# A mixture-of-experts kernel on one core: the last two experts' rows are added to gathered sums and written over the normalised output, an 87-row expert comes last, capacities are finer and expert 1 takes the unsplit path

## The chip, the cores and the metric

The kernel runs on one core of one Trainium2 chip. The metric is the device time of one execution in microseconds (us); the time before is the median of three runs.

## What is computed

One encoder layer runs over two sequences of 1024 and 512 tokens with 1024 features, in fp32: RMSNorm, one projection, a pooling mixer and differential attention, an output projection with a residual, and then a mixture of experts. Every token takes one of four groups and in it two of eight experts, 32 experts in all; an expert's three matrices are 1024x512 (gate, up) and 512x1024 (down).

```python
gates = g_top * (e_top / jnp.sum(e_top, axis=-1, keepdims=True))
eid = g_idx * EXPERTS_PER_GROUP + e_loc
...
hid = jax.nn.silu(xblk @ w_gate[e]) * (xblk @ w_up[e])
return hid @ w_down[e]
...
return h + ff                  # encoder_layer
x = rmsnorm(x, g_final)        # run_trunk, over each token's row
```

With the inputs that are drawn here, experts 0 and 1 get 146 and 41 rows (a row is one token of one expert); the other 30 get, sorted, 249, 248, 203, 195, 185, 158, 149, 139, 124, 106, 103, 97, 87, 84, 75, 71, 66, 61, 59, 58, 55, 53, 52, 49, 46, 33, 27, 24, 19 and 10.

## The kernel before, in words

The first half (mixer, attention, output projection, routing) is not touched. The routing leaves three arrays in DRAM: `hn` (the normalised rows), `acc` (the sums, which start as h) and `tab` (for each expert its tokens and gates).

**The expert stage** (`experts`, L1289) goes through 32 slots. Slots 0 and 1 are experts 0 and 1; behind them `ORDER` lists places in the sorted list of the other 30, the fullest being place 0. `CAPS` gives each place a capacity, that is, how many rows are gathered, multiplied and scattered whatever the true count; what goes over it would be done in extra passes (the loop at L1496), of which there are none here. A capacity is cut into blocks of at most 128 rows. In iteration i the tensor engine (PE) does gate(i), up(i) and down(i-1) (`use`, with `E.proj` L1067 and `E.down` L1078). Weights come in pieces of 1 MB, six for an expert, through eight buffers (`er_raw`) on SP's queue, up to eight pieces ahead.

A capacity of at most `WHOLE` = 64 takes the **whole** path: the weights go unsplit into fp32 matmuls, two side by side in the array's columns (0 and 64), and the two halves are added afterwards. All others are **split**: ACT copies a piece to a rounded high part (L104), DVE subtracts to get the low part (L108), and PE makes three passes (L112 to L114) for a block of over 64 rows, or two (L1113, L1114) for a smaller one. So a matrix costs PE the same time at 96 rows as at 128.

`gather` (L1145) fetches a block's rows from `hn` with an indirect DMA on POOL's queue, two experts ahead. `weigh` (L1187) scales the result by the gate; `scatter` (L1203) adds it to `acc` with an indirect DMA.

**The end** (`close`, L1223). The last `TAIL` = 2 experts (32 rows each) don't reach `acc` in time. Their weighted rows are split in high and low parts and stacked in one tile of 128 rows (`stack`). `tail_step` loads `acc` in six pieces (L1361) behind the last scatter of the third-last expert, and builds a 0/1 matrix `hot` of rows against all 1536 tokens (L1347, L1356). For each of twelve token tiles PE multiplies `hot` with the rows (L1232), DVE adds the product to the sums in two halves (L1236), ACT squares (L1238), the inverse root is taken on POOL for three groups and on DVE for the last, the row is scaled (L1256 on DVE; L1253 on ACT and L1254 on POOL for three tiles) and written out (L1259).

Of the kernel before, what the change touches and what calls it, by code (L numbers as in the profile page):

```python
# [1090 lines left out]
class Block:  # L1091
# [111 lines left out]
    def scatter(self):  # L1203
        self.nc.gpsimd.indirect_dma_start(out=self.E.S["acc"],  # L1204
                                          out_offset=bass.IndirectOffsetOnAxis(ap=self.ix[:self.m, 0:1], axis=0),
                                          in_=self.y[:self.m], in_offset=None, compute_op=OP.add)

    def stack(self, ps, parts):

        self.weigh(ps)  # L1210
        hi, lo = parts[:self.m], parts[self.m:]
        for hf in range(2):
            s = slice(hf * 512, (hf + 1) * 512)
            split_hi(self.nc, hi[:, s], self.y[:self.m, s])
            split_lo(self.nc, lo[:, s], self.y[:self.m, s], hi[:, s])
# [7 lines left out]
def close(nc, E, tail, outs):  # L1223

    accs, gB = tail["acc"], tail["g"]
    stat = E.X([128, FF], F32, "s", bufs=4)
    ss, rr, rt = (stat[:, i * TT:(i + 1) * TT] for i in range(3))

    def add(t):
        ps = [E.bank() for _ in range(2)]  # L1230
        for hf, p in enumerate(ps):
            nc.tensor.matmul(p, lhsT=tail["hot"][:, t * 128:(t + 1) * 128],  # L1232
                             rhs=tail["rows"][:, hf * 512:(hf + 1) * 512], start=True, stop=True)
        for hf, p in enumerate(ps):
            d = accs[t][:, hf * 512:(hf + 1) * 512]
            nc.vector.tensor_tensor(d, d, p, OP.add)  # L1236
            yield
        nc.scalar.activation(E.W([128, D], F32R, "hi"), accs[t], AF.Square, accum_out=ss[:, t:t + 1])  # L1238

    def root(ts, eng):  # L1240
        ts = slice(ts.start, ts.stop)
        if eng is nc.gpsimd:
            eng.tensor_scalar(ss[:, ts], ss[:, ts], 1.0 / D, EPS, op0=OP.mult, op1=OP.add)
            rsqrt_pool(nc, rr[:, ts], ss[:, ts], rt[:, ts])
            return
        nc.vector.tensor_scalar(ss[:, ts], ss[:, ts], 1.0 / D, EPS, op0=OP.mult, op1=OP.add)
        yield
        yield from rsqrt_steps(nc, rr[:, ts], ss[:, ts], rt[:, ts])

    def scale(t):  # L1250
        a, r = accs[t], rr[:, t:t + 1]
        if t in POOLED:
            nc.scalar.activation(a, a, AF.Copy, scale=r)  # L1253
            nc.gpsimd.tensor_tensor(a, a, gB, OP.mult)  # L1254
        else:
            nc.vector.scalar_tensor_tensor(a, a, r, gB, op0=OP.mult, op1=OP.mult)  # L1256
        tok = TGORDER[t // 4] * 512 + t % 4 * 128
        o, row = (outs[0], tok) if tok < NP else (outs[1], tok - NP)
        nc.sync.dma_start(o[row:row + 128], a)  # L1259
        yield  # L1260

    def run(work, side):
        for k, w in enumerate(work):
            for _ in w:
                for _ in range(SIDE if k else 0):
                    next(side, None)
        for _ in side:
            pass

    t0, ready, side = 0, [], iter(())  # L1270
    for w, e in zip(LAST, ROOTS):
        ts = range(t0, t0 + w)
        t0 += w
        run([add(t) for t in ts], side)
        side = root(ts, nc.gpsimd if e else nc.vector)
        if e:
            for _ in side:
                pass
        if t0 < TT:
            run([scale(t) for t in ready], iter(()))  # L1280
        else:
            run([iter(())] + [scale(t) for t in ready], side)
        ready = ts
    run([scale(t) for t in ready], iter(()))
    for b in tail["last"]:
        b.scatter()


def experts(tc, A, S, K, RO, outs):  # L1289
    nc = tc.nc  # L1290
    E = Experts(tc, A, S, K)
    with ExitStack() as ctx:
# [16 lines left out]
        def ids(i):  # L1309
# [33 lines left out]
        def tail_step(k):  # L1343
            if k == 0:
                assert all(b.m == 128 // TAIL // 2 for b in tail["last"])
                tail["pos"] = E.raw()[:, :NT]
                nc.gpsimd.iota(tail["pos"], pattern=[[1, NT]], base=128, channel_multiplier=0,  # L1347
                               allow_small_or_imprecise_dtypes=True)
                tail["g"] = E.rows()
                nc.sync.dma_start(tail["g"], bcast(A["g_final"], D))  # L1350
                tail["to"] = E.X([128, 1], F32, "to")
                nc.vector.tensor_copy(tail["to"], tail["ix"][:, 0:1])
                tail["acc"] = []
            elif k == 1:
                tail["hot"] = E.raw()[:, :NT].bitcast(F32R)
                nc.vector.tensor_scalar(tail["hot"], tail["pos"], tail["to"], None, op0=OP.is_equal)  # L1356
                tail["rows"] = E.rows().bitcast(F32R)
            elif k <= 1 + TT // 2:
                a = E.raw().rearrange("p (t n) -> p t n", t=2)
                o = 128 + (k - 2) * 256  # L1360
                nc.sync.dma_start(a, S["acc"][o:o + 256].rearrange("(t p) n -> p t n", p=128))  # L1361
                tail["acc"] += [a[:, 0], a[:, 1]]
# [24 lines left out]
        def after(d, fn):  # L1387
            todo.append([d, fn])
# [60 lines left out]
        for i in range(n + 1):  # L1449
# [134 lines left out]
```

## Time and profile before

| | us |
|---|---|
| median of three runs (1427.0, 1428.17, 1430.35) | 1428.17 |
| the profiled execution, own time | 1432.71 |
| its span, first to last instruction | 1430.4 |
| PE busy in the span | 1328.7 (93%) |
| DVE, ACT, POOL busy | 828.1, 674.1, 230.4 |
| moved by DMA | 337.94 MB |

The span is what the profile's rows are placed in; the execution's own time holds 2.3 us more around it. A busy share is a mean over stages that have different limits, so rows are read by stage: the expert stage lies at about 700 to 1374 us of the span, the end behind it.

### The profile page before, as it was taken

To read this page: it belongs to the slowest core of one execution; us is meant where nothing else is said; L and a number is where in the kernel's file an instruction comes from. 1 tells how busy PE (TensorE), PEld (TensorE's weight loads), DVE (VectorE), ACT (ScalarE), POOL (GpSimd) and SP (SyncE) were. 2 spreads that over 40 slices of the span, in tenths; PEclk is the share of its full clock that TensorE was granted. 3 is DMA by queue.
4 is the path that set the end of the run, shared out by engine and by line. 5 is a ranking of instruction groups with operands and counts; after the bars stand their busy time and mean duration, and the time that the engine had idled before them with its cause. 6 is when DMAs were issued, how large, how long until landed. Compare 5 with 4: busy or idle time off the path is not lost.

```text
span 1430.4 us, 17564 instructions
## 1 busy us (share of the span) xinstructions
PE 1328.7 (93%) x5986; PEld 926.4 (65%) x5986; DVE 828.1 (58%) x1363; ACT 674.1 (47%) x1039; POOL 230.4 (16%) x376
## 2 busy tenths in 40 slices
PE   7899999988999999998789999999999999999970
PEld 5768888856676668776566656656565666677620
DVE  5495653066988727564766455263444665778354
ACT  6321212166877723221446455363535564777351
POOL 0000000003342210211212111110111122121032
PEclk9999999999999999999799999999999999999985
DMA  8625425436551048312498999898999999999674
GB/s 290 222 103 203 147 103 141 95 77 159 152 136 37 29 170 280 113 60 96 177 365 320 362 325 395 299 383 285 373 368 306 390 364 348 358 386 375 221 281 155
DMA packets 90347, 337.94 MB, mean 236 GB/s; under 512 B 17616, under 2 KB 25296, under 8 KB 65680
## 3 DMA queue, kind: packets, MB, share of 16 engines
q1 hardware_dynamic: 80368, 302.95, 58.3%
q0 software_dynamic: 9312, 29.65, 8.5%
q10 hardware_dynamic: 576, 4.19, 0.8%
q8 instruction: 48, 0.79, 0.2%
q14 instruction: 43, 0.35, 0.1%
HBM read 282.69 MB, written 54.06 MB: 235 GB/s over the span
## 4 chain that ended last, share of the span: by engine, by line
PE 78%; DMA 9%; DVE 5%; ACT 3%; POOL 2%; issue 2%; SPq 0%; POOLq 0%; ACTq 0%; DVEq 0%
PE pm_m L112 8%; PE pm_m L114 8%; PE pm_m L113 8%; PE pm_m L1071 6%; PE pz_z L113 5%; PE pz_z L112 5%; PE pz_z L114 5%; PE ps_sc L393 5%; PE po_o L451 4%; PE pt_t L1129 3%; DMA er_raw<-w_gate 3%; PE ph_h L114 3%; PE ph_h L112 3%; PE ph_h L113 3%; PE pm_m L1083 2%; PE pt_t L438 2%
## 5 line engine op out<-in xcount | busy, mean ns | idle before, releaser
L108 DVE TENSOR_TENSOR ew_lo<-er_raw,ew_hi 128x1024 fp32r<-128x1024 f32 x228 | 272.5, 1219 | 140.9 <-ACT ew_hi L104 140.4
L104 ACT ACTIVATE ew_hi<-er_raw 128x1024 fp32r<-128x1024 f32 x228 | 233.6, 1051 | 45.4 <-DMA er_raw<-w_gate 17.1
L112 PE MATMUL pm_m<-ew_hi,ex_x 128*128 128x512 f32 (+1 forms) x368 | 150.7, 410 | 0.2 <-ACT ex_x L1138 0.2
L113 PE MATMUL pm_m<-ew_lo,ex_x 128*128 128x512 f32 (+1 forms) x368 | 146.8, 399 | 0.0
L114 PE MATMUL pm_m<-ew_hi,ex_x 128*128 128x512 f32 (+1 forms) x368 | 146.6, 398 | 0.2 <-DVE ex_x L1139 0.2
L1204 POOL DMA_INDIRECT acc<-ex_y,ex_ix x40 | 71.7, 1792 | 322.2 <-ACT ex_y L1198 145.9
L112 PE MATMUL pz_z<-xT_hi,w_hi 128*128 128x512 f32 x288 | 115.3, 401 | 8.4 <-ACT xT_hi L153 8.4
L113 PE MATMUL pz_z<-xT_lo,w_hi 128*128 128x512 f32 x288 | 115.3, 401 | 0.0
L114 PE MATMUL pz_z<-xT_hi,w_lo 128*128 128x512 f32 x288 | 113.5, 394 | 0.0
L393 PE MATMUL ps_sc<-st_st 128*128 128x512 f32 x320 | 98.6, 449 | 6.9 <-ACT sm_e L412 5.6
L1071 PE MATMUL pm_m<-er_raw,ex_x 128*64 128x512 f32 (+1 forms) x416 | 96.3, 599 | 0.0
L408 ACT ACTIVATE sm_e<-ps_sc,sb_m 128x1024 f32<-128x1024 f32 x64 | 70.8, 1112 | 38.7 <-PE pt_t L438 37.3
L393 PEld LDWEIGHTS ps_sc<-st_st 128*128 128x128 f32 x320 | 60.5, 196 | 42.7 <-ACT sm_e L408 12.3
L397 DVE TENSOR_REDUCE sb_m<-ps_sc 128x1 f32<-128x1024 f32 x64 | 75.3, 1218 | 21.6 <-PE ps_sc L393 21.6
L112 PEld LDWEIGHTS pm_m<-ew_hi,ex_x 128*128 128x128 f32 (+1 forms) x368 | 66.6, 181 | 32.3 <-ACT ex_x L1138 7.3
L114 PEld LDWEIGHTS pm_m<-ew_hi,ex_x 128*128 128x128 f32 (+1 forms) x368 | 66.6, 181 | 21.1 <-DVE ex_x L1139 0.8
L113 PEld LDWEIGHTS pm_m<-ew_lo,ex_x 128*128 128x128 f32 (+1 forms) x368 | 66.8, 182 | 18.0 <-issue 0.2
L112 PE MATMUL ph_h<-wo_woh,mx_mh 128*128 128x512 f32 x192 | 77.8, 407 | 0.0
L114 PE MATMUL ph_h<-wo_woh,mx_ml 128*128 128x512 f32 x192 | 77.3, 403 | 0.0
L451 PE MATMUL po_o<-wT_wT,v_V 128*128 128x512 f32 x160 | 77.2, 606 | 0.0
L113 PE MATMUL ph_h<-wo_wol,mx_mh 128*128 128x512 f32 x192 | 77.2, 403 | 0.0
L112 PE MATMUL pm_m<-ew_hi,ex_h 128*128 128x512 f32 (+1 forms) x184 | 75.0, 408 | 0.0
(289 smaller groups left out, 2399.8 us busy)
## 6 DMA issues: line engine op xcount, KB each, us to landing
er_raw<-w_gate SPq DMA_DIRECT2D x64, 1024.0 KB
er_raw<-w_up SPq DMA_DIRECT2D x62, 1024.0 KB
er_raw<-w_down SPq DMA_DIRECT2D x62, 1024.0 KB
st_st<-qk SPq DMA_DIRECT2D x48, 256.0 KB
rw_raw<-w_in SPq DMA_DIRECT2D x16, 512.0 KB
rw_raw<-xT SPq DMA_DIRECT2D x12, 512.0 KB
x_x<-x SPq DMA_DIRECT2D x12, 512.0 KB
qk<-rp_h SPq DMA_DIRECT2D x24, 256.0 KB
```

The lines of the kernel that those rows point to most:

```text
L104: nc.scalar.activation(hi, raw, AF.Copy)
L108: nc.vector.tensor_tensor(lo, raw, hi.bitcast(F32), OP.subtract)
L112: nc.tensor.matmul(out, lhsT=xh, rhs=wh, start=first, stop=False)
L113: nc.tensor.matmul(out, lhsT=xh, rhs=wl, start=False, stop=False)
L114: nc.tensor.matmul(out, lhsT=xl, rhs=wh, start=False, stop=last)
L393: nc.tensor.matmul(sc[:, b], lhsT=st[:, cc, 0, q0:q0 + 128], rhs=st[:, cc, i, k0:k0 + 512], start=i == 1, stop=i == 2)
L397: nc.vector.tensor_reduce(m[:, :1], sc, axis=AX.XY, op=OP.max, negate=True)
L408: nc.scalar.activation(e, sc, AF.Exp, bias=m[:, :1], accum_out=acc)
L451: nc.tensor.matmul(self.o, lhsT=V[:, self.t0 // 128 + kt, self.h * 128:(self.h + 1) * 128], rhs=self.wT[:, kt], start=kt == 0, stop=kt == ...
L1071: self.nc.tensor.matmul(p[b.at(k)], lhsT=b.x[:, i * 2 + k], rhs=w[:, k * 512:(k + 1) * 512], start=i == 0, stop=i == 3)
L1129: nc.tensor.transpose(p[0][:, k], src[:m, (k0 + k) * 128:(k0 + k + 1) * 128], self.id[:m, :m])
L1204: self.nc.gpsimd.indirect_dma_start(out=self.E.S["acc"], out_offset=bass.IndirectOffsetOnAxis(ap=self.ix[:self.m, 0:1], axis=0), in_=self. ...
```

## The change

It does five things. (1) Capacities become finer (252 for 256, 60 for 64 and so on; 3264 rows in all for 3616); no block changes its path, but for (2) expert 1, whose capacity goes from 128 to 48, so that it becomes whole. (3) `ORDER` is mixed anew: the last slots are now place 25 (36 rows, whole), place 29 (32 rows, whole) and place 12 (96 rows for 87, split); before they were 7 (160 rows, split), 29 and 28 (32 rows each, whole). (4) The normalisation takes `acc` without the last two experts' rows: twelve tiles are squared, scaled and written as they are. Beside it the rows of `acc` that those 128 slots name are gathered (L1336), PE adds to each the weighted rows of the same token (`same`, `sums`), the sums are normalised and an indirect DMA writes them over the output rows (L1271). That DMA waits for the six writes of the tiles. (5) The output is one array in `acc`'s layout; two token rows a partition are loaded and written at a time.

```diff
-LAST = (2, 3, 4, 3)
...
+LAST = (4, 4, 4)
+PATCH = 1
...
-ORDER = (17, 12, 0, 18, 26, 13, 1, 19, 20, 8, 2, 21, 27, 14, 3, 22, 23, 9, 4, 24, 15, 5, 25, 10, 6, 16, 11, 7, 29, 28)
-CAPS = (256,) * 2 + (224,) * 2 + (192,) + (160,) * 3 + (128,) * 4 + (96,) * 5 + (64,) * 9 + (32,) * 4 + (160, 128)
+ORDER = (17, 13, 0, 18, 26, 14, 1, 19, 20, 8, 2, 21, 27, 15, 3, 22, 9, 4, 23, 16, 5, 24, 10, 6, 28, 11, 7, 25, 29, 12)
+CAPS = (252, 252, 208, 200, 192, 160, 160, 160, 128, 112, 108, 100, 96, 88, 80, 76, 72, 64, 64, 60, 60, 56, 56, 52, 48, 36) + (32,) * 4 + (148, 48)
...
+def close(nc, E, tail, out, finish):
...
+    def same():
+
+        to = tail["to"]
+        p = E.PT([m, m], F32, "t")
+        nc.tensor.transpose(p, to[:m].to_broadcast([m, m]), E.K["ident"][:m, :m])
+        eq = E.W([128, D], F32R, "hi").bitcast(F32)[:m, :m]
+        nc.vector.tensor_scalar(eq, p, to[:m], None, op0=OP.is_equal)
+        return eq
+
+    def sums(eq):
         ps = [E.bank() for _ in range(2)]
...
+        for rhs, lhs in ((tail["old"], E.K["ident"][:m, :m]), (tail["rows"], eq)):
+            for hf, p in enumerate(ps):
+                nc.tensor.matmul(p[:m], lhsT=lhs, rhs=rhs[:m, hf * 512:(hf + 1) * 512], start=rhs is tail["old"],
+                                 stop=rhs is tail["rows"])
+        return ps
+
+    new = tail["old"][:m]
+    c = t = 0
+    for n, w in enumerate(LAST):
+        c0, ts = c, range(t, t + w)
+        t += w
+        for i in ts:
+            nc.scalar.activation(junk, acc[i], AF.Square, accum_out=ss[:, c:c + 1])
+            c += 1
+        if n == 0:
+            finish()
+        if n == PATCH:
+            ps = sums(same())
+            nc.scalar.activation(new[:, :512], ps[0][:m], AF.Square, accum_out=ss[:m, c:c + 1])
+            nc.scalar.activation(new[:, 512:], ps[1][:m], AF.Square, accum_out=rt[:m, 15:16])
+            nc.vector.tensor_tensor(ss[:m, c:c + 1], ss[:m, c:c + 1], rt[:m, 15:16], OP.add)
+            c += 1
+        cs = slice(c0, c)
+        nc.vector.tensor_scalar(ss[:, cs], ss[:, cs], 1.0 / D, EPS, op0=OP.mult, op1=OP.add)
+        rsqrt(nc, rr[:, cs], ss[:, cs], rt[:, cs])
+        for j, i in enumerate(ts):
+            nc.vector.scalar_tensor_tensor(acc[i], acc[i], rr[:, c0 + j:c0 + j + 1], gB, op0=OP.mult, op1=OP.mult)
+            if i % 2:
+                nc.sync.dma_start(rows2(out, i // 2), tail["raw"][i // 2])
+        if n == PATCH:
+            for hf, p in enumerate(ps):
+                s = slice(hf * 512, (hf + 1) * 512)
+                nc.vector.scalar_tensor_tensor(new[:, s], p[:m], rr[:m, c - 1:c], gB[:m, s], op0=OP.mult, op1=OP.mult)
+            for b, o in tail["last"]:
+                b.scatter(tail["rows"][o:o + b.m])
+    nc.gpsimd.indirect_dma_start(out=out, out_offset=bass.IndirectOffsetOnAxis(ap=tail["ix"][:m, 0:1], axis=0),
+                                 in_=new, in_offset=None)
...
+        def tail_load():
+
+            m = tail["m"]
+            tail["old"] = E.rows()
+            nc.gpsimd.indirect_dma_start(out=tail["old"][:m], out_offset=None, in_=S["acc"],
+                                         in_offset=bass.IndirectOffsetOnAxis(ap=tail["ix"][:m, 0:1], axis=0))
+            tail["raw"], tail["acc"] = [], []
+            for j in range(TT // 2):
+                a = E.raw()
+                nc.sync.dma_start(a, rows2(S["acc"], j))
...
                     if i == n - TAIL:
-                        after(DELAY["out"], lambda: at.__setitem__(3, len(stream) + RAW))
+                        tail["rows"] = E.X([128, D], F32, "y")
+                        after(LOAD, tail_load)
                 else:
...
+                    fn = lambda b=b, p=pd[0], to=tail["rows"][o:o + b.m]: b.weigh(p, to)
+                    if i < n:
+                        after(DELAY["out"], fn)
+                    else:
+                        tail["finish"] = fn
```

The first place is PE at slot 1, expert 1's gate and up. In the rows `k_ident` marks a transpose, `k_ind` a small product of the schedule, `ew_hi` and `ew_lo` the two parts of a weight piece, `er_raw` the piece itself, `ex_x` the expert's rows. Before:

```order
L1129 MATMUL pt_t_6184<-k_ident_59,ex_s_6038 128x96 x4
L962 MATMUL pm_m_6195<-k_ind_6096,k_sv_6173 32x64
L112 MATMUL pm_m_6123<-ew_hi_6040,ex_x_6082 128x512
L113 MATMUL pm_m_6123<-ew_lo_6041,ex_x_6082 128x512
L114 MATMUL pm_m_6123<-ew_hi_6040,ex_x_6082 128x512
```

The same place with the change:

```order
L1128 MATMUL pt_t_6137<-k_ident_59,ex_s_6027 128x84 x4
L961 MATMUL pm_m_6148<-k_ind_6073,k_sv_6130 32x64
L1070 MATMUL pm_m_6092<-er_raw_5705,ex_x_6059 48x512 x2
L1070 MATMUL pm_m_6161<-er_raw_5923,ex_x_6059 48x512 x4
L1070 MATMUL pm_m_6161<-er_raw_5925,ex_x_6059 48x512 x4
L1128 MATMUL pt_t_6184<-k_ident_59,ex_xg_6006 128x64 x8
```

Twenty-four passes over split parts become eight unsplit matmuls a matrix, and no high and low parts are made for this expert.

The second place is ACT at the end. Before, the squares (L1238) stand behind the copies of both last experts' rows (L1194, L104), and each waits for DVE's additions:

```order
L1194 ACTIVATE ex_y_11275<-pm_m_11246,ex_ix_10274 32x512 x2
L104 ACTIVATE ex_xg_11165<-ex_y_11275 32x512 x2
L1194 ACTIVATE ex_y_11284<-pm_m_11268,ex_ix_10499 32x512 x2
L104 ACTIVATE ex_xg_11165<-ex_y_11284 32x512 x2
L1238 ACTIVATE ew_hi_11298,ex_s_11291<-er_raw_11209 128x1024
L1238 ACTIVATE ew_hi_11306,ex_s_11291<-er_raw_11209 128x1024
```

With the change (L1193 is place 29's weighing, L1197 place 12's, L1248 the squares of two tiles a row, L1254 and L1255 those of the patched rows):

```order
L1193 ACTIVATE ex_y_11032<-pm_m_11132,ex_ix_10288 32x512 x2
L1248 ACTIVATE ew_lo_11184,ex_s_11062<-er_raw_11046 128x1024 x2
L1248 ACTIVATE ew_lo_11184,ex_s_11062<-er_raw_11048 128x1024 x2
L1197 ACTIVATE ex_y_11032<-pm_m_11154,ex_ix_10465 96x512
L1197 ACTIVATE ex_y_11032<-pm_m_11155,ex_ix_10465 96x512
L1248 ACTIVATE ew_lo_11184,ex_s_11062<-er_raw_11050 128x1024 x2
L1248 ACTIVATE ew_lo_11184,ex_s_11062<-er_raw_11052 128x1024 x2
L1254 ACTIVATE ex_xg_11044,ex_s_11062<-pm_m_11216 128x512
```

Four squares now stand ahead of the last expert's weighing, and none waits for an addition.

The third place is POOL's queue at the end of the change (before, 42 small operations of the inverse roots, three row products and two late scatters stood here):

```order
L1349 MEMSET ex_s_11062 128x16
L1204 DMA acc<-ex_y_11040,ex_ix_10095 1664x1024
L1336 DMA ex_xg_11044<-acc,ex_ix_10467 128x1024
L1204 DMA acc<-ex_y_11032,ex_ix_10465 1664x1024
L1204 DMA acc<-ex_y_11032,ex_ix_10288 1664x1024
L1271 DMA y<-ex_xg_11044,ex_ix_10467 1664x1024
```

Only transfers are left on it; the last one, the patch of the output, ends the kernel's own work.

## Rows read from the trace of the kernel before

**Rows 1.** The page: the span.
```profile
span 1430.4 us, 17564 instructions
```
**Rows 2.** Windows of the expert stage: length, PE, PEld, DVE, ACT, POOL busy, PE clock, DMA.
```profile
850.00:900.00 50.00, 48.00 (x217) 31.62 (x214) 29.16 (x31) 26.61 (x35) 7.32 (x6) 0.97 1.02 385
...
1100.00:1150.00 50.00, 48.34 (x226) 32.90 (x221) 31.71 (x33) 29.90 (x38) 9.48 (x7) 1.00 1.02 384
```
**Rows 3.** Windows of 5 us, same columns.
```profile
868.00:873.00 5.00, 3.00 (x12) 0.81 (x8) 4.32 (x6) 3.74 (x6) 0.00 (x0) 0.76 1.02 342
1352.00:1357.00 5.00, 5.00 (x23) 3.58 (x23) 0.30 (x1) 0.00 (x0) 0.00 (x0) 1.00 1.02 429
```
**Rows 4.** SP's waits, 760 to 1350: us in total, times, longest.
```profile
SPq L1047 <- PE pm_m L1071: 196.1, 36, 16.1
```
**Rows 5.** PE's waits, 840 to 1150: us in total, times, longest.
```profile
PE pt_t L1129 <- DVE ex_x L1139: 6.1, 5, 2.0
PE pm_m L1113 <- DVE ex_x L1139: 1.6, 1, 1.6
```
**Rows 6.** PE in order of time, 1340 to 1431: start, us, operation, count.
```profile
1349.61 0.51 PE L112 MATMUL pm_m<-ew_hi,ex_h 128*128 128x512 f32 x1
...
1359.13 1.91 PE L1071 MATMUL pm_m<-er_raw,ex_x 128*32 128x512 f32 x8
1360.97 0.43 PE L1129 MATMUL pt_t<-k_ident,ex_s 32*128 32x32 f32 x4
1361.33 5.34 PE L1071 MATMUL pm_m<-er_raw,ex_x 128*32 128x512 f32 x24
1366.51 2.74 PE L1083 MATMUL pm_m<-er_raw,ex_h 128*32 128x512 f32 x12
...
1378.11 5.33 PE L1232 MATMUL pm_m<-ex_xg,er_raw 128*128 128x512 f32 x13 [0.67 <-DVE ex_xg L108]
```
**Rows 7.** ACT in order of time at the end.
```profile
1370.64 1.38 ACT L1194 ACTIVATE ex_y<-pm_m,ex_ix 32x512 f32<-32x512 f32 x2 [0.72 <-PE pm_m L1083]
...
1379.34 1.06 ACT L1238 ACTIVATE ew_hi<-er_raw 128x1024 fp32r<-128x1024 f32 x1 [2.71 <-DVE er_raw L1236]
...
1380.54 1.06 ACT L1238 ACTIVATE ew_hi<-er_raw 128x1024 fp32r<-128x1024 f32 x1
```
**Rows 8.** DVE in order of time at the end.
```profile
1404.86 2.19 DVE L77 TENSOR_SCALAR ex_s<-ex_s 128x3 int32<-128x3 int32 x1
...
1408.34 0.16 DVE L82 SCALAR_TENSOR_TENSOR ex_s<-ex_s 128x3 f32<-128x3 f32 x1
1408.54 0.16 DVE L84 SCALAR_TENSOR_TENSOR ex_s<-ex_s 128x3 f32<-128x3 f32 x1
...
1410.98 3.68 DVE L1256 SCALAR_TENSOR_TENSOR er_raw<-er_raw,ex_s,ex_xg 128x1024 f32<-128x1024 f32 x3
```
**Rows 9.** The chain that ended last, two steps: an indirect gather, an indirect scatter.
```profile
713.83 4.42 DMA ex_xg<-hn,ex_ix
...
1368.56 3.83 DMA acc<-ex_y,ex_ix
```
**Rows 10.** SP's queue in order of time: the loads of `acc`, the last writes.
```profile
1372.60 3.16 SPq L1361 DMA_DIRECT2D er_raw<-acc  x6
...
1415.54 0.81 SPq L1259 DMA_DIRECT2D y_prompt<-er_raw  x2
```
**Rows 11.** Windows behind the last write's issue, columns as in group 2.
```profile
1416.00:1420.00 4.00, 0.00 (x0) 0.00 (x0) 0.00 (x0) 0.00 (x0) 0.00 (x0) 0.50 0.68 266
1420.00:1430.00 10.00, 0.00 (x0) 0.00 (x0) 0.00 (x0) 0.00 (x0) 0.00 (x0) 0.50 0.00 0
```
**Rows 12.** Groups by line and shape: fp32 matmuls, side by side and single; busy, mean ns.
```profile
L451 PE MATMUL po_o<-wT_wT,v_V 128*128 128x512 f32 x160 | 77.2, 606 | 0.0
...
L1071 PE MATMUL pm_m<-er_raw,ex_x 128*64 128x512 f32 x288 | 67.1, 601 | 0.0
...
L1071 PE MATMUL pm_m<-er_raw,ex_x 128*32 128x512 f32 x128 | 29.2, 596 | 0.0
```

More of the change, by code (lines that the diff above doesn't have):

```diff
@@ L1201, in weigh, with scatter @@
                 nc.vector.scalar_tensor_tensor(d, p[:m], self.gate[:m], d, op0=OP.mult, op1=OP.add)
-    def scatter(self):
+    def scatter(self, y=None):
+        y = self.y[:self.m] if y is None else y
         self.nc.gpsimd.indirect_dma_start(out=self.E.S["acc"],
                                           out_offset=bass.IndirectOffsetOnAxis(ap=self.ix[:self.m, 0:1], axis=0),
[L1206 to L1215, printed above, removed]
+                                          in_=y, in_offset=None, compute_op=OP.add)
@@ L1218, in slots @@
 def slots():
     return [(NE - STATIC + e, e) for e in range(STATIC)] + [(j, None) for j in ORDER]
[L1223 to L1229, printed above, removed]
-        ps = [E.bank() for _ in range(2)]
[L1231 to L1286, printed above, removed]
@@ L1290, in experts @@
+def experts(tc, A, S, K, RO, out):
     nc = tc.nc
@@ L1321, in ids @@
             if i == n - 1:
-                tail["last"] = [b for j in range(n - TAIL, n) for b in blocks[j]]
+                o, tail["last"] = 0, []
                 tail["ix"] = E.X([128, 2], I32, "ix", bufs=12)
-                for j in range(2 * TAIL):
-                    b = tail["last"][j // 2]
-                    nc.sync.dma_start(tail["ix"][j * b.m:(j + 1) * b.m], b.src)
+                for b in [b for j in range(n - 1, n - TAIL - 1, -1) for b in blocks[j]]:
+                    assert o % 32 == 0 and o + b.m <= 128
+                    nc.sync.dma_start(tail["ix"][o:o + b.m], b.src)
+                    tail["last"].append((b, o))
+                    o += b.m
+                tail["m"] = o
         def gather(i):
@@ L1341, in experts @@
         at = [0, 0, 0, SOON]
[L1343 to L1362, printed above, removed]
+        def tail_load():
[7 more added lines that the diff above has]
+                nc.sync.dma_start(a, rows2(S["acc"], j))
+                tail["raw"].append(a)
+                tail["acc"] += [a[:, :D], a[:, D:]]
+            tail["g"] = E.rows()
+            nc.sync.dma_start(tail["g"], bcast(A["g_final"], D))
+            tail["to"] = E.X([128, 1], F32, "to")
+            nc.vector.tensor_copy(tail["to"][:m], tail["ix"][:m, 0:1])
+            tail["stat"] = E.X([128, FF], F32, "s", bufs=4)
+            nc.gpsimd.memset(tail["stat"][:, :16], 0.0)
         def fetch(k, queue=None):
-            while len(stream) <= at[0] < k:
-                tail_step(at[0] - len(stream))
-                at[0] += 1
             while at[0] < min(k, len(stream)):
@@ L1481, in experts @@
                     if i == n - TAIL:
-                        after(DELAY["out"], lambda: at.__setitem__(3, len(stream) + RAW))
-                else:
-                    to = tail["rows"][(i - n + TAIL - 1) * 128 // TAIL:][:128 // TAIL]
-                    after(DELAY["stack"], lambda b=blocks[i - 1][0], p=pd[0], to=to: b.stack(p, to))
+                        tail["rows"] = E.X([128, D], F32, "y")
+                        after(LOAD, tail_load)
+                else:
+                    (b, o), = [v for v in tail["last"] if v[0] is blocks[i - 1][0]]
+                    fn = lambda b=b, p=pd[0], to=tail["rows"][o:o + b.m]: b.weigh(p, to)
[3 more added lines that the diff above has]
+                        tail["finish"] = fn
         while todo:
             tick()
-        fetch(len(stream) + 2 + TT // 2)
-        close(nc, E, tail, outs)
+        ctx.enter_context(tc.manual_schedule(engines={ET.PE, ET.DVE, ET.Activation, ET.SP, ET.Pool}))
+        close(nc, E, tail, out, tail["finish"])
     with ExitStack() as ctx:
@@ L1576 @@
          for n, a in arrays.items()}
[L1577 to L1578 removed]
+    out = nc.dram_tensor("y", [NT + 128, D], F32, kind="ExternalOutput").ap()
     with tile.TileContext(nc) as tc:
[L1580 removed]
+        build(tc, A, out)
     r = run(nc, [arrays], core_ids=[0])
[L1582 to L1583 removed]
+    got = r.results[0]["y"].reshape(NT + 128, D)
+    y = np.concatenate([got[place(i):place(i) + 128] for i in range(TT)])
+    return y[:NP].reshape(1, NP, D), y[NP:].reshape(1, NS, D)
```

32 lines of the change are left out of this document (14 added, 18 removed).

## Prediction

> **What bounds the kernel now.** I read the span first, then windows of the expert stage, the waits of PE and of the weight queue, and last the order of time at the end. The span is 1430.4 us [rows 1]. Of the two 50 us windows shown, PE is busy for 48.0 and 48.34 although the transfers move 385 and 384 GB/s and are busy throughout [rows 2]; the other windows between 750 and 1350 are like these or full. So PE bounds the expert stage, with the weights close behind. Where PE does stand still, it waits for the copies of rows or weights that stand behind a late weight piece: six waits, 6.1 and 1.6 us together [rows 5], one of them followed by a mean granted clock of 0.76, a mixture of the 1.2 and 2.4 GHz levels [rows 3]. They fall behind pairs of whole experts, which use up six pieces in the PE time of four. Yet the transfers have room: alone on the rings the weights run at 429 GB/s [rows 3], and their queue spent 196.1 us waiting for PE to free a buffer of a whole expert [rows 4].
>
> The end is different. The third-last expert's down begins at 1349.61, and the two whole experts' matmuls follow from 1359.13 [rows 6]. From there to the end of the span are 1430.4 - 1359.1 = 71.3 us, of which PE needs 15; behind that PE has only the 24 small products with `hot`, and the end is a chain on DVE with ACT and POOL: additions, squares, roots, scalings. One DVE root step takes 2.19 us there and the same kind 0.16 us elsewhere [rows 8]; the slow one ran beside a row product on POOL. The last two writes are issued from 1415.54 [rows 10]; bytes move until about 1420 and nothing in the 10 us behind it, which are the empty passes and the program's close [rows 11].
>
> **The change, part by part.** A split block's down is 40 passes from 1349.61 to 1359.13, or 0.238 us a pass [rows 6]; a matrix of a split block of over 64 rows is 24 passes, 5.7 us. Whole matmuls lie two side by side: (67.1 + 29.2) / 416 = 0.2315 us a row of the trace [rows 12], 16 a matrix, 3.7 us. So a whole expert costs PE 3 x 2.0 = 6.0 us less than a split one.
>
> *Expert 1 becomes whole:* -6.0 us, on the path, since PE bounds this stretch. It also takes 12 high and 12 low parts from ACT and DVE, which are covered, so nothing more. Its buffers are now freed by PE instead of by a split, later by some us each; the buffered pieces cover that. The schedule's products now stand among shorter matmuls, and PE may wait for DVE between them: 0 to 2 us, I take +1.0.
>
> What speaks against this part is the switching between arrangements of the array: transposes and schedule products stand among the paired matmuls. In the trace four transposes among them take from 1360.97 to 1361.33, both switches included [rows 6], so nothing is added. The Trainium skill (TensorEngine Tiling, key properties) says that changing the tiling mode drains the engine. A drain of one matmul's length less its spacing, 0.60 - 0.23 us [rows 12], at some ten switches would be 3.7 us and put the sum at 1416; by the row it is none.
>
> *The order:* the expert that is last now is split and runs behind the third-last one's down, where before there were two whole ones. Counted to the moment at which the third-last down is done (call it z), PE has 6.0 us less to do; the same 6.0 come back behind z, below. The pair 22, 23 is taken apart, and with it goes the 1.6 us wait that follows it [rows 5]: -1.6. Three pairs stay, and their waits with them; a new pair (expert 1 and place 17) stands at the start, where pieces were fetched ahead.
>
> *Finer capacities:* no block loses a pass. Transposes become a little shorter (four take 0.43 us at 32 rows [rows 6]): 0 to -2 us over all blocks, I take -1.0. 352 rows fewer are gathered and as many fewer scattered, 2.9 MB; that costs nothing on the path while PE bounds it.
>
> To z: -6.0 + 1.0 - 6.0 - 1.6 - 1.0 = **-13.6 us**.
>
> *The end, counted from z.* PE: gate and up of place 12, down of 29, down of 12, with transposes: 5.7 + 5.7 + 3.7 + 5.7 + 0.9 = 21.7. Beside it the third-last expert's rows are weighed (1.38 [rows 7]) and scattered (3.83 [rows 9]); at about 5.6 the six loads of `acc` may start, 2.5 us each at 429 GB/s. Four land by 17; two wait for buffers that are freed at 14 to 16, and land by 22, `g_final` by 23. ACT: weighing of 29 from 16.0 to 17.4, four squares at 1.20 [rows 7] to 22.2, weighing of 12 to 23.6, four more squares to 28.4. DVE, which starts at 22.2: eleven small steps at 0.20 [rows 8] to 24.4, four scalings at 3.68 / 3 = 1.23 to 29.3, a comparison to 29.5. Now PE multiplies the rows with it, two fp32 matmuls of 0.965 us (77.2 / 80 [rows 12]); in this stage 13 passes took 5.33 us, 0.41 for 0.238 [rows 6], so 1.7 times as long: to 32.8. Squares of the patched rows to 33.8, roots to 36.0, four scalings to 40.9, the two half rows to 42.2, roots to 44.4, four scalings to 49.3. The last write then takes what it takes now, some 4 us [rows 10, 11], and 1.2 for twice the bytes: 54.5. Only then may the patch go: an indirect transfer takes 3.83 to 4.42 us [rows 9], I take 4.4 for its 128 rows: 58.9. With the 10.4 us behind the last byte: 69.3, against 71.3: **-2.0 us**. POOL no longer works beside DVE, so I count no step of 2.19 us. Bounds: -5 (the products at the full clock, the patch quicker) to +5 (loads or `g_final` late, the patch at twice its price). The two late scatters into `acc` and the gather for the patch are covered by DVE's scalings.
>
> **The sum:** -13.6 - 2.0 = -15.6 us. The profiled execution took 1432.71 us and would take 1417.1; against the median of the runs, 1428.17, that is **1412.6 us**. The bounds of the terms (to z -9 to -17, the end -5 to +5) reach from 1406 to 1424.
>
> **Rivals.**
> *Uneven blocks over fewer engines.* Suppose an indirect transfer is dealt to a number of engines that divides its rows: 124 = 4 x 31 and 76 = 4 x 19 go over four engines instead of sixteen. At 429 / 16 = 26.8 GB/s for one engine [rows 3], 31 rows of 4 KB take 4.7 us and 8 rows 1.2: 3.5 us more, four times (gather and scatter of places 0 and 1), and 1.7 twice: 17.4 us in which a weight piece waits for its slowest engine. For it: the waits lie around just these experts. Against: weights are fetched up to eight pieces ahead. Half of it would be felt: 1421.3. All row counts of the trace are multiples of 32, so it shows nothing of this. The Trainium skill (DMA: Bandwidth & Descriptors, why a DMA increments its semaphore by 16) gives this rule, the largest divisor up to 16, and names an exception for some direct copies on POOL's path; no run here shows it yet.
>
> *The weights take over.* PE's time is saved, but it waits for pieces instead: only the end's 2.0 us remain, 1426.2. For it: transfers busy throughout in [rows 2]. Against: the 196.1 us of [rows 4], and 429 GB/s against 384.
>
> *The side-by-side pairs break (slower).* Eight experts now have whole blocks of 60, 56, 52, 48 or 36 rows; the trace shows pairs of 64 and of 32 alone [rows 12]. If a count that fills no strip of the array kept the second matmul waiting, a row of the trace would cost 77.2 / 160 = 0.4825 us as a single one does, 0.251 more, 48 times an expert: 12 us, 96 in all, 1509. It decides as soon as one uneven expert's pair costs over 0.28 us a row (-15.6 is then used up). Against: 64 and 32 rows cost the same, so not the count sets the time but the position.
>
> *An expert overflows,* and the change's own case is not met: by the counts given above the tightest capacities are 148 for 146, 60 for 58 and 252 for 249, so a token or two that is routed otherwise on the chip could do it. An extra pass (six pieces, 14.7 us) and a second normalisation (6 MB to load, 14.7, and twelve scalings, 14.8) would add some 44 us: 1457.
>
> **How the numbers follow.** Forecast 0.72, uneven blocks 0.14, weights 0.08, broken pairs 0.04, overflow 0.02. The range 1405 to 1424 holds the forecast with its bounds and the uneven blocks; the rest is 0.14. A measurement of this kernel tells about 0.2% from no change, that is 2.9 us: faster is below 1425.3. Forecast and uneven blocks but for their upper ends give 0.84, the weights and those ends 0.10, the two slow cases 0.06.
>
> **What would show it.** Expert 1's gate and up each take 3.7 us; matmuls of 60 columns keep 0.23 us a row; waits behind three pairs only; z some 13.6 us earlier; from z to the end 69, with about 21.7 of PE in it, DVE idle once for some 4 us between the first and second group of four, and one indirect write behind the last tile's write. Wrong would be: new waits for weights around places 0 and 1, loads of `acc` that land after DVE is ready, or a patch that takes much over 4.4 us.

## The result, and the profile after

The change made the kernel slower: 1440.27 us (median of 5 runs, 1435.84 to 1441.82) beside 1430.35 of the kernel before on the same chip, a ratio of 1.0069 with a 95% interval from 1.0048 to 1.0090. Forecast was 1412.6, a range of 1405 to 1424; the time lies outside it, on the other side of no change.

Call z, as the prediction does, the moment at which the third-last expert's down is done. In the profiled executions:

| | z, us | z to the end of the span | span |
|---|---|---|---|
| before [rows 6, 1] | 1359.1 | 71.3 | 1430.4 |
| forecast | 1345.5 | 69.3 | 1414.8 |
| after | 1361.4 | 75.3 | 1436.7 |

So both halves failed: 15.9 us up to z, 6.0 us behind it.

**Up to z.** The windows of after, columns as in [rows 2]:

```profile
750.00:800.00 50.00, 42.30 (x167) 19.82 (x166) 24.75 (x27) 26.80 (x36) 9.50 (x8) 0.83 1.02 343
...
850.00:900.00 50.00, 44.56 (x202) 25.46 (x199) 29.61 (x31) 29.32 (x39) 8.59 (x5) 0.93 1.00 373
...
950.00:1000.00 50.00, 42.21 (x182) 28.07 (x183) 21.85 (x23) 19.43 (x26) 8.03 (x6) 0.90 0.94 327
...
1100.00:1150.00 50.00, 50.00 (x232) 34.92 (x230) 26.89 (x28) 27.32 (x36) 11.67 (x8) 1.00 0.96 347
```

PE stands still for 5 to 8 us in three windows in which the transfers are busy for 94% of the time or more, and its mean granted clock falls with it (0.83 to 0.93). The last window is full, where before it had the wait behind the pair that was taken apart [rows 2, 5]. PE in order of time shows its four longest waits there (in brackets: idle time and what ended it):

```profile
780.80 0.73 PE L111 MATMUL pm_m<-ew_hi,ex_x 128*88 128x512 f32 x1 [2.61 <-ACT ew_hi L103]
...
791.91 1.09 PE L1128 MATMUL pt_t<-k_ident,ex_xg 124*128 124x124 f32 x4 [2.79 <-DVE ex_x L1138]
...
879.78 1.09 PE L1128 MATMUL pt_t<-k_ident,ex_xg 124*128 124x124 f32 x4 [5.44 <-DVE ex_x L1138]
...
969.45 0.80 PE L1128 MATMUL pt_t<-k_ident,exa_xg 80*128 80x80 f32 x4 [7.79 <-DVE ex_x L1138]
```

The short waits of [rows 5], 2.0 us at most, have not gone: two have grown to 5.44 and 7.79. Behind the last one the clock is at its lower level, 1.2 GHz, for more than 5 us:

```profile
965.00:970.00 5.00, 0.55 (x4) 0.55 (x4) 3.65 (x6) 3.52 (x5) 3.30 (x2) 0.53 0.95 326
970.00:975.00 5.00, 5.00 (x15) 1.43 (x15) 5.00 (x7) 3.23 (x6) 0.00 (x0) 0.50 0.95 259
```

What PE waits for is a copy of rows that stands behind the copy of a weight piece, and that piece is late. ACT makes the first half of both copies (DVE adds the low parts behind it); ACT in order of time:

```profile
876.80 1.06 ACT L103 ACTIVATE ew_hi<-er_raw 128x1024 fp32r<-128x1024 f32 x1 [3.32 <-DMA er_raw<-w_gate]
877.77 0.58 ACT L1137 ACTIVATE ex_x<-pt_t 128x512 fp32r<-128x512 f32 x1
...
962.76 2.00 ACT L103 ACTIVATE ew_hi<-er_raw 128x1024 fp32r<-128x1024 f32 x2 [9.13 <-DMA er_raw<-w_gate]
```

The piece that ACT takes at 962.76 was issued at 944.93, 17.8 us before; in experiment 2 below, where these blocks have 128 rows, the same piece is issued at 932.41 and taken at 944.42, 12.0 us later. What the pieces share the engines with is seen on POOL, which issues the row transfers (order of time):

```profile
753.75 1.52 POOL L1204 DMA_INDIRECT acc<-ex_y,exa_ix  x1 [0.36 <-DVE ex_y L1200]
755.57 0.93 POOL L1148 DMA_INDIRECT ex_xg<-hn,ex_ix  x1 [0.30 <-PE pt_t L1128]
779.06 1.51 POOL L1204 DMA_INDIRECT acc<-ex_y,ex_ix  x1 [22.55 <-DMA acc<-ex_y,exa_ix]
...
854.59 3.26 POOL L1204 DMA_INDIRECT acc<-ex_y,ex_ix  x1 [5.91 <-ACT ew_hi L103]
882.42 1.44 POOL L1204 DMA_INDIRECT acc<-ex_y,ex_ix  x1 [24.58 <-DMA acc<-ex_y,ex_ix]
```

The scatter issued at 854.59 is that of place 0's 124 rows. It lands 27.1 us after its issue; that of the same expert's 128 rows, issued at 847.09, took 6.6. Place 1's lands after 24.3 us. Even the 64-row scatter of 753.75 is slow (24.5 us), with a gather of 124 rows just ahead of it on the queue. While the 124 rows move, the row queue q0 shows 512 packets for 0.51 MB (861 to 882; all of them lie between 861.6 and 881.4, so the rows move for 19.8 us, and place 1's for 18.6); in before 128 rows are 144 packets for 0.52 MB (852 to 860):

```profile
q0 software_dynamic: 512, 0.51, 13.1%
```

```profile
q0 software_dynamic: 144, 0.52, 33.8%
```

**Behind z.** PE, SP's queue, DVE and POOL of after in order of time:

```profile
1361.39 0.47 PE L111 MATMUL pm_m<-ew_hi,ex_x 128*96 128x512 f32 x1
...
1383.12 0.28 PE L1229 MATMUL pt_t<-k_ident,ex_to 128*128 128x128 f32 x1
1384.16 1.98 PE L1238 MATMUL pm_m<-ex_xg,k_ident 128*128 128x512 f32 x4 [0.77 <-DMA ex_xg<-acc,ex_ix]
1399.26 3.40 PE L1238 MATMUL pm_m<-ex_y,ew_hi 128*128 128x512 f32 x4 [13.11 <-DVE ew_hi L1231]
```

```profile
1373.93 3.13 SPq L1341 DMA_DIRECT2D er_raw<-acc  x6
1377.11 0.44 SPq L1345 DMA_DIRECT2D ex_xg<-g_final  x1
```

```profile
1384.52 0.17 DVE L1259 TENSOR_SCALAR ex_s<-ex_s 128x4 f32<-128x4 f32 x1 [6.87 <-ACT ew_lo L1248]
...
1393.98 4.87 DVE L1262 SCALAR_TENSOR_TENSOR er_raw<-er_raw,ex_s,ex_xg 128x1024 f32<-128x1024 f32 x4 [7.32 <-DMA ex_xg<-g_final]
...
1403.41 0.16 DVE L1256 TENSOR_TENSOR ex_s<-ex_s 128x1 f32<-128x1 f32 x1 [4.30 <-ACT ex_xg L1255]
...
1414.12 4.87 DVE L1262 SCALAR_TENSOR_TENSOR er_raw<-er_raw,ex_s,ex_xg 128x1024 f32<-128x1024 f32 x4
```

```profile
1368.17 1.43 POOL L1204 DMA_INDIRECT acc<-ex_y,ex_ix  x1 [6.97 <-DMA acc<-ex_y,ex_ix]
...
1424.14 0.99 POOL L1271 DMA_INDIRECT y<-ex_xg,ex_ix  x1 [23.80 <-DMA y<-er_raw]
```

PE needs the 21.7 us that were forecast (1361.39 to 1383.12), and DVE starts its first roots at z + 23.1 (forecast 22.2). Then it waits 7.32 us for `g_final` (the weights of the last normalisation, one row), which was to land at z + 23 and lands at z + 32.6. The first scaling, forecast at z + 24.4, is so 8.2 us late. The steps from there to the patch keep their forecast lengths; from the patch's start to the end of the span it is 12.6 us where 14.8 was forecast, which gives 2.2 of the 8.2 back.

### The profile page after: what moved, and what is told of

Its sections match the earlier page's. It is cut to its first block, busy times and chain, and to the rows that moved or that the text cites. A ratio compares the mean times of both kernels' runs of the same rounds, so it can differ in the third digit from the quotient of the medians.

```text
span 1436.7 us, 17366 instructions
## 1 busy us (share of the span) xinstructions
PE 1317.4 (92%) x5947; PEld 896.9 (62%) x5947; DVE 799.4 (56%) x1350; ACT 653.7 (46%) x1025; POOL 220.7 (15%) x333
## 5 line engine op out<-in xcount | busy, mean ns | idle before, releaser
L107 DVE TENSOR_TENSOR ew_lo<-er_raw,ew_hi 128x1024 fp32r<-128x1024 f32 x216 | 257.7, 1218 | 172.5 <-ACT ew_hi L103 172.3
L103 ACT ACTIVATE ew_hi<-er_raw 128x1024 fp32r<-128x1024 f32 x216 | 219.9, 1049 | 54.5 <-DMA er_raw<-w_gate 28.0
L111 PE MATMUL pm_m<-ew_hi,ex_x 128*128 128x512 f32 (+9 forms) x352 | 143.0, 406 | 3.6 <-ACT ew_hi L103 3.6
L112 PE MATMUL pm_m<-ew_lo,ex_x 128*128 128x512 f32 (+9 forms) x352 | 140.1, 398 | 1.3 <-DVE ew_lo L107 1.3
L113 PE MATMUL pm_m<-ew_hi,ex_x 128*128 128x512 f32 (+9 forms) x352 | 140.2, 398 | 0.0
L1070 PE MATMUL pm_m<-er_raw,ex_x 128*32 128x512 f32 (+6 forms) x448 | 104.0, 599 | 0.6 <-ACT ex_x L1133 0.6
L111 PEld LDWEIGHTS pm_m<-ew_hi,ex_x 128*128 128x128 f32 (+9 forms) x352 | 60.8, 173 | 39.3 <-ACT ew_hi L103 12.1
L112 PEld LDWEIGHTS pm_m<-ew_lo,ex_x 128*128 128x128 f32 (+9 forms) x352 | 60.9, 173 | 21.8 <-DVE ew_lo L107 2.1
L113 PEld LDWEIGHTS pm_m<-ew_hi,ex_x 128*128 128x128 f32 (+9 forms) x352 | 60.7, 172 | 21.4 <-issue 0.5
L111 PE MATMUL pm_m<-ew_hi,ex_h 128*128 128x512 f32 (+10 forms) x176 | 71.2, 404 | 0.0
## 6 DMA issues: line engine op xcount, KB each, us to landing
er_raw<-w_up SPq DMA_DIRECT2D x62, 1024.0 KB, 12.6
er_raw<-w_down SPq DMA_DIRECT2D x62, 1024.0 KB, 11.9
```

The source lines that it names most:

```text
L103: nc.scalar.activation(hi, raw, AF.Copy)
L107: nc.vector.tensor_tensor(lo, raw, hi.bitcast(F32), OP.subtract)
L111: nc.tensor.matmul(out, lhsT=xh, rhs=wh, start=first, stop=False)
L112: nc.tensor.matmul(out, lhsT=xh, rhs=wl, start=False, stop=False)
L113: nc.tensor.matmul(out, lhsT=xl, rhs=wh, start=False, stop=last)
L1070: self.nc.tensor.matmul(p[b.at(k)], lhsT=b.x[:, i * 2 + k], rhs=w[:, k * 512:(k + 1) * 512], start=i == 0, stop=i == 3)
```

## The experiments

Ratios are to the kernel before, run on the same chip, with 95% intervals. The first four ran on one chip, the next four on a second, the last three on a third.

**1. All counts multiples of 16.**

```
-CAPS = (252, 252, 208, 200, 192, 160, 160, 160, 128, 112, 108, 100, 96, 88, 80, 76, 72, 64, 64, 60, 60, 56, 56, 52, 48, 36) + (32,) * 4 + (148, 48)
+CAPS = (256, 256, 208, 208, 192, 160, 160, 160, 128, 112, 112, 112, 96, 96, 80, 80, 80) + (64,) * 7 + (48, 48) + (32,) * 4 + (160, 48)
```

> Every capacity of the changed kernel is rounded up to a multiple of 16 (252 to 256, 200 to 208, the 124-, 84-, 108-, 100-, 88-, 76-, 72-, 60-, 56-, 52- and 36-row blocks gone); order, whole expert 1 and end as in the change. Theory 'few engines' (a row transfer is dealt to the largest number of engines up to 16 that divides its rows): the scatters of places 0 and 1, which took 27.1 us to land and kept POOL waiting 22 to 25 us three times, take under 8 us; PE's stalls in the expert stage fall from 23 us to under 8; the down of the third-last expert ends 14 to 16 us earlier than 1361.4, and the time is 1422 to 1428. Theory 'weights bind' (PE's saving cannot be had, because the weight pieces already set the pace): the stalls only move, and the time stays within 3 us of the change, 1437 to 1443.

Measured: 1427.14 us, 0.9992 (0.9972 to 1.0013). The time did not stay: "weights bind" in that form falls. Two of the expectations are missed: z is at 1349.8, 11.6 us earlier and not 14 to 16, and PE's waits from 740 to z fall from 22.3 to 10.4 us, not under 8.

**2. Only 252 to 256.**

```
-CAPS = (252, 252, 208, ...
+CAPS = (256, 256, 208, ...
```

> Only the two largest capacities go from 252 to 256, so that blocks of 124 rows become 128; the 76-row block of one other expert and all other uneven counts stay. Theory 'few engines': 124 = 4 x 31 is the worst of the counts by far (31 rows in a row on one engine, 19 for 76, at most 10 for the rest), so this gives two thirds or more of what the multiples of 16 give: 1425 to 1431. Theory 'weights bind': within 3 us of the change. A third theory, that any count that is no multiple of 16 or 32 costs by itself: under half of the first run's gain, since only 2 of 16 uneven counts are mended.

Measured: 1424.25 us, 0.9962 (0.9940 to 0.9984), just below the expected range. The two 124-row blocks are the whole of it; mending the other uneven counts too (experiment 1) gained nothing more. PE's waits, columns as above:

```profile
784.53 0.66 PE L1128 MATMUL pt_t<-k_ident,ex_xg 128*128 128x128 f32 x4 [2.65 <-DVE ex_x L1138]
...
867.75 0.66 PE L1128 MATMUL pt_t<-k_ident,ex_xg 128*128 128x128 f32 x4 [1.70 <-DVE ex_x L1138]
...
951.22 0.50 PE L1128 MATMUL pt_t<-k_ident,exa_xg 80*128 80x80 f32 x4 [2.07 <-DVE ex_x L1138]
```

The last two are the places of 879.78 and 969.45 above: 12.0 and 18.2 us earlier. z is at 1343.6, 17.8 before that of the change and 15.5 before that of the kernel before, where 13.6 was forecast. The time gains less, 15 us: the last stretch, behind the patch's start, is 3.4 us longer in this program (the last section has the numbers). Here the 128 rows in the place of the 124 move for 7.1 us (852.6 to 859.7) and 5.1 us (933.1 to 938.2).

**3. `g_final` first.**

```
             m = tail["m"]
+            tail["g"] = E.rows()
+            nc.sync.dma_start(tail["g"], bcast(A["g_final"], D))
             tail["old"] = E.rows()
...
-            tail["g"] = E.rows()
-            nc.sync.dma_start(tail["g"], bcast(A["g_final"], D))
```

> The changed kernel with the load of the final weights (g_final) issued ahead of the gather and of the six loads of acc instead of behind them; nothing else. Theory 'the weights row stands last in line': the 7.3 us in which DVE waits before its first scaling go, and the time falls by 5 to 7 us, to 1433 to 1435. Rival: the same bytes have to pass, so the squares of the second group come as much later and the first scaling starts less than 3 us earlier: 1437 to 1440.

Measured: 1432.67 us, 1.0023 (1.0005 to 1.0040), just below the expected range. `g_final` is now issued at 1361.61, 13 us ahead of the loads of `acc`, since it need not wait for the scatter as they do. From z (1361.1) to the end of the span (1429.6) it is 68.5 us, where 69.3 was forecast; that they agree so well is in part luck, since the first scaling is 1.9 us late and the last stretch 2.3 us short. The first scaling follows its roots with no wait:

```profile
1385.19 0.17 DVE L1259 TENSOR_SCALAR ex_s<-ex_s 128x4 f32<-128x4 f32 x1 [7.51 <-ACT ew_lo L1248]
...
1387.37 4.87 DVE L1262 SCALAR_TENSOR_TENSOR er_raw<-er_raw,ex_s,ex_xg 128x1024 f32<-128x1024 f32 x4
```

**4. The kernel before with the new capacities alone.** In `before`, `CAPS` is that of the change with `(148, 128)` at its end.

> The kernel before with the new capacities alone (expert 1 stays at 128 rows and split; old order and old end). Theory 'few engines': 12 to 18 us slower than before, 1441 to 1447, with new PE stalls near places 0 and 1. Theory 'weights bind': fewer bytes of rows are moved, so no change or up to 2 us faster than before.

Measured: 1430.43 us, 1.0002 (0.9979 to 1.0025): neither. Its profile has waits of 7.14 us (at 878.81) and 7.61 us (at 969.32), though that execution was the longest of its twelve. Experiment 8 takes it up.

**5. The changed kernel again,** unaltered.

> The changed kernel itself, unaltered, beside the other three of this group on one chip, since it was timed on another chip than the first four experiments. If the group of before and the chips are comparable, 0.5 to 0.9% slower than before; if the difference to the run with 256 rows came from the chip, it would be within 0.3% of before.

Measured: 1440.77 us, 1.0070 (1.0048 to 1.0092). The result stands on a second chip, and against it the repairs are worth 1.0070 - 0.9962, 15 us, for the 256 rows, and 1.0070 - 1.0023, 6.7 us, for `g_final` (ratios from two chips, each to the kernel before on its own).

**6. Both repairs,** the edits of 2 and 3.

> The changed kernel with both repairs: the two largest capacities 256 in place of 252, and g_final loaded ahead of acc. If the two causes are separate (row transfers over four engines in the expert stage, the late row of weights at the end), the gains add: about 15 us from the first and 6 from the second, 1417 to 1421 and faster than both kernels. Rival: the end then waits for the loads of acc instead, and the second gain is under 2 us: 1423 to 1426. The forecast of 1412.6 would be reached only if nothing else was wrong in it.

Measured: 1418.42 us, 0.9925 (0.9900 to 0.9949). The gains add, and the version beats both kernels.

**7. 126 + 126 rows.**

```
-                m = min(128, cap - o)
+                m = 126 if cap == 252 else min(128, cap - o)
```

> The changed kernel with the 252 rows of places 0 and 1 cut into 126 + 126 instead of 128 + 124; same rows, same capacities, same number of transfers. If the largest divisor up to 16 sets the number of engines, 126 = 14 x 9 goes over 14 engines, 9 rows each, and costs about as little as 128: the scatters land in under 9 us and the time is within 3 us of the run with 256 (0.3 to 0.6% faster than before). If any count that is no multiple of 4, 8 or 16 is slow, both blocks are slow now, and it is slower than the change.

Measured: 1424.14 us, 0.9966 (0.9942 to 0.9990), the time of 256 rows (z at 1345.0, 1.4 us behind experiment 2). The scatter of place 0's second block is waited for from 850.45 to 863.89, 13.4 us (14.4 with 128 rows in experiment 2, 27.8 with 124); so longer than the 9 us expected, but the same as for 128. Of these its 126 rows move for 6.5 us. Uneven by itself is not slow. The row queue, 856.3 to 862.8:

```profile
q0 software_dynamic: 160, 0.52, 40.2%
```

**8. Experiment 4 with 256.**

> The kernel before with the finer capacities, but 256 for the two largest. The kernel before with all of them (252 too) came out level with before, although its profile has the stalls of 7.1 and 7.6 us behind 124-row transfers. If these stalls cost there what they cost in the change, something else in the finer capacities must give about as much back: then this run is 0.4 to 0.9% faster than before. If the kernel before hides the slow transfers, it is within 0.2% of before.

Measured: 1425.78 us, 0.9955 (0.9936 to 0.9975). So the 124 rows cost the kernel before 6.7 us too, and the finer capacities without them give it 6.4 us, which is why experiment 4 came out level. Where these lie is seen in its windows against [rows 2]: PE busy 49.51 in place of 48.34 at the last pair. The starts of the same instruction in both profiles fall apart in steps of 1 to 2.5 us at the three pairs near 955, 1040 and 1121, and by 1.9 us more in small steps from there to z. The window of the last pair here:

```profile
1100.00:1150.00 50.00, 49.51 (x232) 32.65 (x230) 30.17 (x34) 29.82 (x40) 10.83 (x7) 1.00 1.02 371
```

**9. 127 rows.** `CAPS` begins with 256, 255.

> The changed kernel with 256 rows for place 0 and 255 for place 1, so that one block has 127 rows, a prime. One look. If the largest divisor up to 16 sets the number of engines, all 127 rows go over one engine; the 124-row scatters took 18.5 to 19.8 us for 31 rows on an engine, 0.6 us a row, so this one takes about 76 us, the gather ahead of it 20 to 40, PE stands still for 30 to 70 us around place 1, and the run takes 1460 to 1500 us. If an uneven block only costs because it is no multiple of 4, 8 or 16, it costs what one 124-row block does: 1428 to 1436.

Measured, a single run: 1479.21 us. POOL in order of time, and q0 from 957.5 to 1026:

```profile
949.40 4.73 POOL L1204 DMA_INDIRECT acc<-ex_y,ex_ix  x1 [5.62 <-ACT ex_s L1176]
1026.65 1.46 POOL L1204 DMA_INDIRECT acc<-ex_y,ex_ix  x1 [72.52 <-DMA acc<-ex_y,ex_ix]
```

```profile
q0 software_dynamic: 2048, 0.54, 5.4%
```

One row less than 128, and the next scatter waits 77.3 us for this one; its rows move for 67.9 of them (957.7 to 1025.6). PE waits 18.61 us at 868.66 and 30.28 us at 1028.44, and from 1000 to 1028 transfers are busy for 6% of the time: one of sixteen engines.

**10. Both repairs, expert 1 split.** Experiment 6 with `(148, 128)` at the end of `CAPS`.

> The kernel with both repairs, but with expert 1 at 128 rows and split, as in the kernel before. The forecast counted 5 us for the whole expert 1 (6.0 of PE time less 1.0 of waits): if so, this is 4 to 6 us slower than with it, 0.9955 to 0.9965 of before. Rival: its weights come no earlier, and the PE time that it saves is waited away at the next pieces (a wait of 3.2 us stands at 783 to 786 in the repaired kernel and none in the kernel before): within 2 us of it, 0.991 to 0.994.

Measured: 1415.55 us, 0.9894 (0.9865 to 0.9924), so no slower than with it whole, and the 4 to 6 us that the forecast asked for are not there; the intervals overlap, and which of the two is better stays open. The two profiles can't decide it: this one reaches the expert stage 9.0 us ahead of experiment 6 (711.36 against 720.38, the first rows of expert 0), before expert 1's first matmul, is only 2.5 us ahead at z, and has a last stretch 4.0 us shorter. It has the lowest time of the study.

**11. Experiment 8 with expert 1 whole,** `(148, 48)`.

> The kernel before (old order, old end) with the finer capacities, 256 for the two largest, and expert 1 whole. Against the same kernel with expert 1 split (0.9955) it prices the whole expert 1 a second time: 5 us faster by the forecast (0.992), within 2 us by the rival (0.994 to 0.997). Against the kernel with both repairs (0.9925) it prices the new order and end together: the forecast had 9.6 us for these.

Measured: 1424.58 us, 0.9939 (0.9916 to 0.9963), some 2 us from experiment 8, with overlapping intervals: nearer to the rival's price than to the forecast's. Against experiment 6 (0.9925) it puts the new order and end together at 2 us, where the forecast had 9.6. By the profiles the order gives more, z at 1342.9 in experiment 6 against 1354.4 here, and the end nothing, 72.3 us from z there against 70.9 here. PE in order of time, first here, then in experiment 8 (the rows are the same transposes and matmuls):

```profile
780.43 0.66 PE L1129 MATMUL pt_t<-k_ident,ex_xg 128*128 128x128 f32 x4
...
786.03 1.08 PE L1129 MATMUL pt_t<-k_ident,ex_xg 128*128 128x128 f32 x4 [3.93 <-DVE ex_x L1139]
787.03 1.98 PE L1083 MATMUL pm_m<-er_raw,ex_h 128*64 128x512 f32 x4
```

```profile
788.44 0.66 PE L1129 MATMUL pt_t<-k_ident,ex_xg 128*128 128x128 f32 x4
...
790.03 0.66 PE L1129 MATMUL pt_t<-k_ident,ex_xg 128*128 128x128 f32 x4
790.62 1.08 PE L1083 MATMUL pm_m<-er_raw,ex_h 128*64 128x512 f32 x4
```

Behind expert 1 it leads by 8.0 us (1.9 of them from a shorter wait at 719, ahead of expert 1). A wait of 3.93 us at the end of the new pair leaves 3.6, and by 1062, behind waits of 2.36 (at 870.20) and 2.00 (at 954.65), the same instruction starts 1.6 us later than in experiment 8.

## Why the prediction was wrong

*Uneven blocks over fewer engines: the rival held, at the wrong price.* The step of the sum that failed is that the finer transfers cost "nothing on the path while PE bounds it"; the rival that doubted it mis-sized it by "31 rows of 4 KB take 4.7 us", an engine's share of the full rate, 26.8 GB/s. Measured, beside the weight loads, 124 rows (31 on an engine, by the rule below) move for 18.6 and 19.8 us, 127 rows (all on one) for 67.9, 126 rows (9 on each) for 6.5 and 128 rows (8 on each) for 5.1 and 7.1: 0.5 to 0.9 us for each row on one engine, whatever the count. So the price was to be had from a row transfer's own time, times the ratio of rows per engine, and not from the rings' rate. Second, "fetched up to eight pieces ahead" did not cover it: the weight piece of 944.93 reached ACT 17.8 us after its issue in place of 12.0, and ACT stood idle for it for 9.13 us in place of 3.29 (experiment 2). Third, PE loses more than it waits, since behind the longest wait the granted clock stays at its lower level for over 5 us (0.50 from 970 to 975). In place of 8.7 us felt, 15. The Trainium skill ("DMA: Bandwidth & Descriptors", "Why a DMA increments its semaphore by 16 and not by 1") has the rule: the number of engines is the largest divisor up to 16. Experiments 2, 7 and 9 agree: 128 and 126 are quick, 124 slow, 127 slowest. The exception that it names for direct copies, which would have spread 127, did not show in these indirect ones.

*The end: right but for one step,* "at about 5.6 the six loads of `acc` may start ... and land by 22, `g_final` by 23". The loads went out at z + 12.5: the third-last expert's rows were weighed at z + 3.5, but their scatter stood on POOL until the one before it had landed, went out at z + 6.8 (1368.17) and took 5.6 us. The prediction's own rows could have told it: in the kernel before the same loads go out at 1372.60 [rows 10], z + 13.5. The gather of the old rows shares the rings with them, and each 1 MB landed 14 to 16 us after its issue. `g_final`, one row for all partitions, was last in line and cost 7.32 us; the kernel before issues it at 1351.41, 21 us ahead of its loads of `acc`. With it first (experiment 3) the end is 68.5 us. The chain of squares, roots, sums and scalings was forecast rightly. The patch landed 3.3 us after its issue, where 4.4 was taken, and the stretch behind it was shorter too. Against before the end is 4.0 us longer, inside its bounds of -5 to +5; the term to z, +2.3 for -9 to -17, is what left the range.

*Expert 1 whole, -6.0 and +1.0: no gain seen.* The matmuls cost what was forecast: 15.2 us for the 64 of the two 48-row experts' gate and up in the groups below (expert 1 is one of them), 3.8 a matrix. The sentence that failed is that a new pair "stands at the start, where pieces were fetched ahead". The profile of experiment 11 shows the lead waited away at the new pair and the two behind it, and experiment 10 finds no gain by time. This speaks for the rival "the weights take over", for this term alone; the intervals don't settle it.

*Finer capacities, -1.0: too small.* Without the 124 rows they gave 6.4 us (experiment 8). "That costs nothing on the path while PE bounds it" does not hold at the pairs, where most of the gain lies. That fewer row bytes let the late weight pieces land sooner there is argued, not shown.

*The order* held: no wait is left where the pair 22, 23 was, and z in experiment 2 is 15.5 us earlier, though seemingly from other parts than forecast (finer capacities more, expert 1 less). By time, order and end together came out at 2 us in experiment 11 for the forecast's 9.6, with overlapping intervals; what they are worth stays open.

*Side-by-side pairs* did not break. The groups by shape of after:

```profile
L1070 PE MATMUL pm_m<-er_raw,ex_x 128*48 128x512 f32 x64 | 15.2, 600 | 0.6 <-ACT ex_x L1133 0.6
L1070 PE MATMUL pm_m<-er_raw,ex_x 128*56 128x512 f32 x64 | 15.0, 600 | 0.0
...
L1070 PE MATMUL pm_m<-er_raw,ex_x 128*60 128x512 f32 x64 | 14.8, 600 | 0.0
```

60 rows cost 14.8 / 64 = 0.231 us, as 64 and 32 do [rows 12]. No second normalisation stands in the profile after, so no expert overflowed. Two slips in these rivals change nothing: the 15.6 us are used up at 0.27 us a row and not at 0.28 (15.6 / 384 on top of 0.2315), and 160 rows for 158 are as tight as the capacities named.

Together: forecast 0.989 of before, measured 1.007. The 124 rows account for 15 us of these 25 and `g_final` for 5 to 7. With both repaired (experiment 6) the time is 5 us above the forecast; 3.4 of these are the longer last stretch of that program, whose cause is open, and the rest is within the intervals. That expert 1's missing gain and the finer capacities' larger one nearly cancel fits the runs but is not resolved by them.

## What to carry to other kernels

Before a row count of an indirect transfer is trimmed, write down its largest divisor up to 16: 126 rows moved in about the time of 128, 124 took about three to four times as long, 127 some ten to thirteen times. A shorter transfer can be the slower one, and it is paid by what shares the engines and the queue with it, here weight pieces and the next scatters. PE time that is saved counts only where the next weights are already there; and at the end of a program, a small load that everything needs goes ahead of the large ones and of what they wait for.

## What the runs showed of the hardware

- q0's packets fit the number of engines k: 512 for 124 rows and 2048 for 127, where 128 rows take 144. If each of 16 rings gets a packet for every row of the fullest one, and one more, k is 4, 1 and 16 (16 x 31 + 16 = 512, 16 x 127 + 16 = 2048, 16 x 8 + 16 = 144). The 160 of 126 rows in experiment 7 fit k = 14 (16 x 9 + 16). The added packets hold next to nothing: the megabytes are those of the rows.
- The last stretch was not alike in all programs: from the patch's start to the end of the span it is 12.6 us in after (from 1424.14) and in experiment 5, 12.5 in experiment 3, 11.9 and 12.0 in experiments 7 and 10, but 16.0 in experiments 1, 2 and 6. Once the patch's bytes have moved the engines and transfers stand all but idle there (1428 to 1436 in after: 2 GB/s), and the cause stays open. Differences of time between these programs hold up to 4 us of it.
- Single executions of one kernel spread more than the differences here: 1420.66 to 1437.34 over twelve runs of experiment 4. Two profiles therefore locate a difference; the medians size it.
